# Eight of 22 up-projection chunks per layer as seven block products (Strassen's scheme), with the modulation columns of layer 0's MLP begun at the 15th chunk

## The chip, the cores and the metric

The kernel runs on one core of a Trainium2 chip. The metric is the device time of one execution in microseconds (us). TensorE (PE) multiplies matrices, VectorE (DVE) and ScalarE (ACT) do elementwise work, GpSimd (POOL) does little here, and SyncE (SP) issues nearly all DMAs. Each engine works through its own instruction list in order.

## What is computed

Two layers of a decoder trunk over 512 tokens of width 1024, all in float32. Each layer has an attention part with three head groups and a gated MLP. The change touches the MLP alone, whose reference is:

```python
h = rmsnorm(x, g_mlp[layer]) * (1.0 + scale2) + shift2
up = h @ w_up[layer]                               # 1024 -> 2 x 2816
u, g = up[..., :D_FF], up[..., D_FF:]
g = causal_depthwise_conv(g, conv_w[layer], conv_b[layer])     # width 3
x = x + gate2 * ((jax.nn.silu(g) * u) @ w_down[layer])
```

`shift`, `scale` and `gate` come from `mod = silu(c) @ w_mod[layer] + b_mod[layer]`: six times 1024 numbers per layer, which the kernel computes as 48 columns of 128.

## The kernel before, in words

Activations are held transposed: features on the 128 partitions, the 512 tokens along the free axis. `h` is eight tiles (k = 0 to 7) of 128 features. Every float32 operand of a matmul is split into a high part (`fp32r`, copied by ACT) and a low part (the rest, subtracted by DVE); a product is three matmuls, high x high (`hh,whi`), low x high (`hl,whi`), high x low (`hh,wlo`), in `mm3` (lines 250 to 253).

The up-projection runs over 22 chunks of 128 features. A chunk has a gate product (`pg`) and an up product (`pu`), each 8 k-tiles x 3 matmuls with 512 columns: 48 matmuls. The class `Weights` streams the weights in the order of the list `plan`: a DMA of 128x1024 into one of three `raww` buffers (line 148), ACT's copy to `whi` (L174), DVE's subtraction to `wlo` (L186), with two buffers for each of `whi` and `wlo`. `pump` is called between matmuls and starts these steps for the next weight. `post` (lines 888 to 906) finishes a chunk: ACT scales `pg` with the last tap of the convolution (L890), DVE adds the other taps (L892, L895), ACT applies SiLU (L898), DVE multiplies by `pu` (L902), and ACT and DVE split the result (L240, L242) for the down-projection (`dps`), which follows after chunk 21. Chunk 0 is different: it is computed in two halves of 256 tokens, between the steps that make `h` (L297, L299, L300).

In layer 0 another generator runs beside this: `mod_gen`, 56 columns (the last 8 of layer 0, the gate of its MLP, and all 48 of layer 1). One column is a 512 KB DMA (`rawm`, two buffers) and one DVE instruction of 128x1024 (L217). In the kernel before it starts with the MLP, and is moved on by `tick()` about four columns a chunk.

The generators only record the instructions. A scheduler then sets the order on each engine, by priorities and by its own estimates, so the order on an engine isn't that of the code.

## Time and profile before

| | us |
|---|---|
| median of three runs (1326.34 to 1332.99) | 1330.62 |
| the profiled execution | 1329.34 |
| its span, first to last instruction | 1327.6 |
| TensorE busy in the span | 1276.8 |
| DVE busy | 849.8 |
| ACT busy | 642.6 |
| layer 0's chunks, first `post` to last `post` | 318.89 to 553.98 |
| layer 1's chunks, first `post` to last `post` | 960.40 to 1178.43 |

The busy time of TensorE counts matmuls that overlap in the pipeline, so a matmul of 512 columns is listed with some 390 ns while the next one starts about 230 ns later. How fast TensorE goes is read from the starts. DVE and ACT instructions also start a little before the one ahead has ended, when nothing else holds them.

### The profile page before, as it was taken

To read this page: it belongs to the slowest core of one execution; us is meant where nothing else is said; L and a number is where in the kernel's file an instruction comes from. 1 tells how busy PE (TensorE), PEld (TensorE's weight loads), DVE (VectorE), ACT (ScalarE), POOL (GpSimd) and SP (SyncE) were. 2 spreads that over 40 slices of the span, in tenths; PEclk is the share of its full clock that TensorE was granted. 3 is DMA by queue.
4 is the path that set the end of the run, shared out by engine and by line. 5 is a ranking of instruction groups with operands and counts; after the bars stand their busy time and mean duration, and the time that the engine had idled before them with its cause. 6 is when DMAs were issued, how large, how long until landed. Compare 5 with 4: busy or idle time off the path is not lost.

```text
span 1327.6 us, 17720 instructions
## 1 busy us (share of the span) xinstructions
PE 1276.8 (96%) x6568; PEld 1057.6 (80%) x6568; DVE 849.8 (64%) x1600; ACT 642.6 (48%) x1158; POOL 22.1 (2%) x16
## 2 busy tenths in 40 slices
PE   4999999999999999999999999999999999999997
PEld 2788778787877788888898888878888888888886
DVE  6789999859888864422357788876754444443232
ACT  5667677745333333322346687785543333333231
POOL 5100000000000000000000000000000000000000
PEclk8999999999999999999999999999999999999999
DMA  9455464434888853333422334212133333332331
GB/s 370 167 165 157 145 189 136 132 99 144 260 270 265 271 170 95 92 88 99 129 87 96 96 100 141 77 43 90 48 111 97 95 95 95 96 91 88 104 99 64
DMA packets 56601, 174.39 MB, mean 131 GB/s; under 512 B 8130, under 2 KB 10450, under 8 KB 56516
## 3 DMA queue, kind: packets, MB, share of 16 engines
q1 hardware_dynamic: 55364, 172.16, 41.4%
q8 instruction: 52, 0.85, 0.3%
q10 hardware_dynamic: 1088, 1.05, 0.2%
q14 instruction: 33, 0.27, 0.1%
q0 software_dynamic: 64, 0.06, 0.0%
HBM read 159.41 MB, written 2.10 MB: 122 GB/s over the span
## 4 chain that ended last, share of the span: by engine, by line
PE 55%; DMA 7%; DVE 7%; ACT 4%; issue 3%; SPq 0%; DVEq 0%; ACTq 0%
DMA rawm<-in_wmod_dram 7%; PE dps L251 6%; PE dps L253 6%; PE dps L252 6%; PE pu L251 4%; PE pu L253 4%; PE pu L252 4%; PE pg L252 4%; PE pg L253 4%; PE pg L251 4%; PE qkps L251 1%; PE qkps L252 1%; PE qkps L253 1%; DVE rawm L217 1%; DVE wlo L186 1%
## 5 line engine op out<-in xcount | busy, mean ns | idle before, releaser
L186 DVE TENSOR_TENSOR wlo<-raww,whi 128x1024 fp32r<-128x1024 f32 (+3 forms) x188 | 224.4, 1194 | 240.9 <-ACT whi L174 236.4
L174 ACT ACTIVATE whi<-raww 128x1024 fp32r<-128x1024 f32 (+3 forms) x188 | 194.4, 1035 | 324.8 <-PE dps L252 137.7
L252 PE MATMUL pg<-hl,whi 128*128 128x512 f32 (+1 forms) x368 | 143.1, 389 | 1.5 <-DVE hl L300 1.5
L253 PE MATMUL pu<-hh,wlo 128*128 128x512 f32 (+1 forms) x368 | 141.3, 384 | 3.1 <-DVE wlo L186 3.0
L251 PE MATMUL pg<-hh,whi 128*128 128x512 f32 (+1 forms) x368 | 141.5, 385 | 1.6 <-ACT whi L174 1.6
L251 PE MATMUL pu<-hh,whi 128*128 128x512 f32 (+1 forms) x368 | 142.4, 387 | 0.1
L253 PE MATMUL pg<-hh,wlo 128*128 128x512 f32 (+1 forms) x368 | 140.9, 383 | 1.1 <-DVE wlo L186 1.1
L252 PE MATMUL pu<-hl,whi 128*128 128x512 f32 (+1 forms) x368 | 140.7, 382 | 0.0
L251 PE MATMUL dps<-mh,whi 128*128 128x512 f32 x308 | 121.5, 394 | 0.0
L253 PE MATMUL dps<-mh,wlo 128*128 128x512 f32 x308 | 121.5, 394 | 0.0
L252 PE MATMUL dps<-ml,whi 128*128 128x512 f32 x308 | 121.2, 393 | 0.0
L217 DVE CUSTOM_DVE_ANT_0 rawm<-rawm,scb,bm 128x1024 f32<-128x1024 f32 x80 | 102.4, 1281 | 23.3 <-DMA rawm<-in_wmod_dram 22.9
L654 ACT ACTIVATE e<-e,nm 128x256 f32<-128x256 f32 (+3 forms) x160 | 89.0, 557 | 33.1 <-DVE nm L641 29.5
L251 PE MATMUL qkps<-hh,whi 128*128 128x512 f32 x224 | 95.3, 426 | 4.7 <-ACT qk L434 4.1
L898 ACT ACTIVATE y<-y 128x512 f32<-128x512 f32 x44 | 27.8, 632 | 147.6 <-DVE y L895 147.6
L253 PE MATMUL qkps<-hh,wlo 128*128 128x512 f32 x224 | 90.2, 403 | 0.0
L252 PE MATMUL qkps<-hl,whi 128*128 128x512 f32 x224 | 90.1, 402 | 0.0
L253 PEld LDWEIGHTS pu<-hh,wlo 128*128 128x128 f32 x368 | 69.1, 188 | 22.2 <-DVE wlo L186 7.0
L641 DVE CUSTOM_DVE_ANT_0 e<-s,cst 128x256 f32<-128x256 f32 (+3 forms) x160 | 76.6, 482 | 11.1 <-PE s L628 3.4
L252 PEld LDWEIGHTS pg<-hl,whi 128*128 128x128 f32 x368 | 69.0, 188 | 17.7 <-DVE hl L300 3.2
L253 PEld LDWEIGHTS pg<-hh,wlo 128*128 128x128 f32 x368 | 69.0, 187 | 16.6 <-DVE wlo L186 1.9
L251 PEld LDWEIGHTS pg<-hh,whi 128*128 128x128 f32 x368 | 69.1, 188 | 16.0 <-ACT whi L174 2.0
(176 smaller groups left out, 2651.2 us busy)
## 6 DMA issues: line engine op xcount, KB each, us to landing
raww<-in_wup_dram SPq DMA_DIRECT2D x88, 512.0 KB
rawm<-in_wmod_dram SPq DMA_DIRECT2D x80, 512.0 KB
raww<-in_wqk_dram SPq DMA_DIRECT2D x32, 512.0 KB
raww<-in_wdown_dram SPq DMA_DIRECT2D x32, 512.0 KB
mu<-in_wmod_dram SPq DMA_DIRECT2D x16, 512.0 KB
raww<-in_wout_dram SPq DMA_DIRECT2D x16, 448.0 KB
raww<-in_wv_dram SPq DMA_DIRECT2D x12, 512.0 KB
raww<-in_wdown_dram SPq DMA_DIRECT2D x16, 384.0 KB
```

The costliest lines, as they stand in the source:

```text
L174: A.activation(out=h[:, 0:m], in_=self.raw[i][:, c:c + m], func=AF.Copy)
L186: V.tensor_tensor(out=lo[:, 0:m], in0=raw[:, c:c + m], in1=h[:, 0:m].bitcast(F32), op=ALU.subtract)
L217: V.tensor_tensor_reduce(out=raw, in0=raw, in1=scb, scale=1.0, scalar=bm[:, l, ci:ci + 1], op0=ALU.mult, op1=ALU.add, accum_out=dst)
L251: T.matmul(ps[:, c], w[0], rhs[0][:, c], start=first, stop=False, skip_group_check=True)
L252: T.matmul(ps[:, c], w[0], rhs[1][:, c], start=False, stop=False, skip_group_check=True)
L253: T.matmul(ps[:, c], w[1], rhs[0][:, c], start=False, stop=last, skip_group_check=True)
L641: anchor[0] = V.tensor_tensor_reduce(out=e[:, 0:n], in0=s[:, 0:n], in1=cst[:, mask + SEQ - n:mask + SEQ], scale=-scale, scalar=3e38, op0=A ...
L654: anchor[1] = A.activation(out=e[:, 0:n], in_=e[:, 0:n], func=AF.Exp, bias=nm, scale=-1.0, accum_out=den).ins
L898: last_silu[0] = A.activation(out=y, in_=y, func=AF.Silu).ins
```

## The change

For chunks 3, 4, 6, 7, 9, 10, 12 and 13 of each layer (`SCH`) the gate and the up weight of the chunk are taken as a 2 x 2 block matrix, A11 and A12 the two halves of the gate weight over k, A21 and A22 those of the up weight, and `h` as 2 x 2 blocks over k-half and token-half (`LO` and `HI`). Seven products of half size replace the eight. Each has 4 k-tiles x 3 matmuls with 256 columns, 84 matmuls in place of 48.

- The seven left factors are A11, A11+A21, A21+A22+A11, A22, A21+A22, A12, and A12+(A21+A22+A11), called f0 to f6 below. `form` makes each: DVE adds (`s3`, `s1`, `s2`, `s4`, L176), ACT's copy of the high part (L189), DVE's subtraction (L190). High and low part of a factor share one tile `wst`. The four buffers of `whi` and `wlo` are used in turn, so a factor needs the buffer of the factor four ahead of it.
- The right factors that are sums of blocks of `h` are made once a layer by `tforms`, from chunk 0 on: for each of four pairs of k-tiles two sums (`hf`, L998), four half-width differences (`td`, `te`, L1005), and two splits (`th`, `tl`, L306 and L308).
- `seven` runs the products P0 to P6 (with f0 to f6). Some are accumulated on top of others in the same half of a PSUM tile; copies of the parts in between are kept by ACT (`k1`, `k2`, L1038, L1040, L1042), and three DVE instructions join the rest (L1044, L1046, L1048). P0 is copied before P2 is added to it, P1 before P3, P2 before P4, and P4 is read by L1046 before P6 goes to the same half.
- Layer 0's `mod_gen` is no longer added at the start of the MLP but ahead of chunk 14 (`max(SCH) + 1`).

```diff
-        plan += [(wup[l, j], 1024, "wp") for j in range(2 * FC)]
+        for c in range(FC):
+            if c in SCH:
+                plan += [((wup[l, 2 * c + 1], wup[l, 2 * c]), f, "st") for f in range(7)]
+            else:
+                plan += [(wup[l, j], 1024, "wp") for j in (2 * c, 2 * c + 1)]
...
+        def form(self, i):
...
+            if f == 1:
+                add("s3", a11, a21)
+            elif f == 2:
+                add("s1", a21, a22)
+                add("s2", s["s1"], a11)
+            elif f == 6:
+                add("s4", a12, s["s2"])
...
+            t = wp.tile([128, 4 * VZ], F32R, tag=("whi", "wlo")[self.par], name="wst")
+            self.par ^= 1
+            A.activation(out=t[:, 0:512], in_=src, func=AF.Copy)
+            V.tensor_tensor(out=t[:, 512:1024], in0=src, in1=t[:, 0:512].bitcast(F32), op=ALU.subtract)
...
+        def tforms():
+            for kp in range(KC // 2):
+                a, b = h[kp], h[kp + KC // 2]
+                f = []
+                for hi, lo in (a, b):
+                    f.append(tmp("hf", "ev"))
+                    V.tensor_tensor(out=f[-1], in0=hi.bitcast(F32), in1=lo.bitcast(F32), op=ALU.add)
+                    yield
+                td, te = tmp("td", "ev"), tmp("te", "ev")
+                for out, p, q, op in ((td[:, LO], f[0][:, LO], f[0][:, HI], ALU.subtract),
+                                      (td[:, HI], f[0][:, HI], f[1][:, HI], ALU.subtract),
+                                      (te[:, LO], td[:, HI], f[0][:, LO], ALU.subtract),
+                                      (te[:, HI], f[1][:, LO], te[:, LO], ALU.add)):
+                    V.tensor_tensor(out=out, in0=p, in1=q, op=op)
+                    yield
...
+        def seven(c):
...
+            def prod(d, rhs, start=False):
+                w = W.use()
+                for k in range(KC // 2):
+                    hi, lo = w[:, 128 * k:128 * k + 128], w[:, 512 + 128 * k:640 + 128 * k]
+                    rh, rl = rhs(k)
+                    T.matmul(d, hi, rh, start=start and k == 0, stop=False, skip_group_check=True)
+                    T.matmul(d, hi, rl, start=False, stop=False, skip_group_check=True)
+                    T.matmul(d, lo, rh, start=False, stop=k == KC // 2 - 1, skip_group_check=True)
...
+            k1, k2 = tmp("k1", "e"), tmp("k2", "e")
+            prod(pg[:, HI], plain(0, LO), True)
+            A.activation(out=k1[:, LO], in_=pg[:, HI], func=AF.Copy)
+            prod(pu[:, LO], tform(1), True)
+            A.activation(out=k1[:, HI], in_=pu[:, LO], func=AF.Copy)
+            prod(pg[:, HI], tform(2))
+            A.activation(out=k2[:, LO], in_=pg[:, HI], func=AF.Copy)
+            prod(pu[:, LO], tform(3))
+            V.tensor_tensor(out=pu[:, LO], in0=pu[:, LO], in1=k2[:, LO], op=ALU.subtract)
+            prod(pg[:, HI], tform(0))
+            V.tensor_tensor(out=pu[:, HI], in0=k1[:, HI], in1=pg[:, HI], op=ALU.subtract)
+            prod(pg[:, LO], plain(1, LO))
+            V.tensor_tensor(out=pg[:, LO], in0=pg[:, LO], in1=k1[:, LO], op=ALU.add)
+            prod(pg[:, HI], plain(1, HI))
+            g = post(c, pg, [pu])
...
+            if l == 0 and c == max(SCH) + 1:
+                aux.append(mod_gen([(0, u) for u in range(40, 48)] + [(1, u) for u in range(48)], 200))
+            if c in SCH:
...
+                seven(c)
+                continue
             if c == 0:
...
+                aux.append(tforms())
                 continue
...
-                if l == 0:
-                    aux.append(mod_gen([(0, u) for u in range(40, 48)] + [(1, u) for u in range(48)], 200))
                 nst = layer_mlp(l, mp, nst)
...
+SCH = (3, 4, 6, 7, 9, 10, 12, 13)
```

What the scheduler makes of it is shown at three places of layer 0. Rows of the changed kernel have its own line numbers. In the names, the number behind a tile tells one buffer's use from another.

**DVE at the end of chunk 0, before.** Ahead of and behind the last low part of `h` (`hl_3506`) stand two modulation columns (L217), and then the weights of chunk 1.

```order
L297 SCALAR_TENSOR_TENSOR ht_3597<-x_98,scl_108,rstd_3363 128x256
L300 SCALAR_TENSOR_TENSOR hl_3497<-ht_3590,modc_107,hh_3496 128x256
L217 ISA rawm_3484,modc_107<-rawm_3484,scb_96,bm_102 128x1024
L217 ISA modc_107 128x1
L300 SCALAR_TENSOR_TENSOR hl_3506<-ht_3597,modc_107,hh_3505 128x256
L217 ISA rawm_3549,modc_107<-rawm_3549,scb_96,bm_102 128x1024
L217 ISA modc_107 128x1
L186 TENSOR_TENSOR wlo_3633<-raww_3628,whi_3632 128x1024
```

After:

```order
L366 SCALAR_TENSOR_TENSOR hl_3491<-ht_3578,modc_107,hh_3490 128x256
L998 TENSOR_TENSOR hf_3633<-hh_3368,hl_3369 128x512
L366 SCALAR_TENSOR_TENSOR hl_3500<-ht_3585,modc_107,hh_3499 128x256
L998 TENSOR_TENSOR hf_3642<-hh_3392,hl_3393 128x512
L1005 TENSOR_TENSOR td_3649<-hf_3633 128x256
L1005 TENSOR_TENSOR td_3649<-hf_3633,hf_3642 128x256
L1005 TENSOR_TENSOR te_3650<-td_3649,hf_3633 128x256
L240 TENSOR_TENSOR wlo_3621<-raww_3616,whi_3620 128x1024
```

The two modulation columns are gone; the first two sums of `tforms` (L998), and then three of its half-width steps, stand in their place ahead of the weight.

**DVE where chunk 2 ends, before.** The post-processing of chunk 2 (`y_3767`), the modulation columns and the up weight of chunk 3 (`wlo_3822`) take turns.

```order
L892 SCALAR_TENSOR_TENSOR y_3767<-pg_3725,cw_103,y_3767 128x511
L217 ISA rawm_3755,modc_107<-rawm_3755,scb_96,bm_102 128x1024
L217 ISA modc_107 128x1
L895 SCALAR_TENSOR_TENSOR y_3767<-pg_3725,cw_103,y_3767 128x510
L217 ISA rawm_3775,modc_107<-rawm_3775,scb_96,bm_102 128x1024
L217 ISA modc_107 128x1
L902 TENSOR_TENSOR y_3767<-y_3767,pu_3769 128x512
L186 TENSOR_TENSOR wlo_3822<-raww_3773,whi_3821 128x1024
L242 TENSOR_TENSOR ml_3826<-y_3767,mh_3825 128x512
```

After, up to the third factor of chunk 3 (`wst_3870` is f2, `wst_3873` f3, `wst_3907` f5; `tl_3849` and `tl_3853` are the last low parts of the right factors, the first for P1 and P4, the second for P2 and P3):

```order
L1005 TENSOR_TENSOR td_3837<-hf_3830,hf_3835 128x256
L190 TENSOR_TENSOR wst_3873<-raww_3733,wst_3873 128x512
L1005 TENSOR_TENSOR te_3838<-td_3837,hf_3830 128x256
L308 TENSOR_TENSOR ml_3843<-y_3783,mh_3842 128x512
L1005 TENSOR_TENSOR te_3838<-hf_3835,te_3838 128x256
L308 TENSOR_TENSOR tl_3849<-td_3837,th_3848 128x512
L176 TENSOR_TENSOR s1_3866<-raww_3733 128x512
L308 TENSOR_TENSOR tl_3853<-te_3838,th_3852 128x512
L176 TENSOR_TENSOR s2_3868<-s1_3866,raww_3735 128x512
L190 TENSOR_TENSOR wst_3907<-raww_3735,wst_3907 128x512
L176 TENSOR_TENSOR s4_3923<-raww_3735,s2_3868 128x512
L190 TENSOR_TENSOR wst_3870<-s2_3868,wst_3870 128x512
```

The last steps of `tforms` stand behind the end of chunk 2 (the product with `pu_3785` is just ahead of these rows), and f5 ahead of f2. On TensorE the products of this chunk stand in the order P0, P1, P3, P2, P4, P5, P6.

**ACT in a later pair (chunks 6 and 7), before.** The copies of weights (L174) and the post-processing of these chunks:

```order
L174 ACTIVATE whi_4118<-raww_4065 128x1024
L890 ACTIVATE y_4104<-pg_4061,cb_104,cw_103 128x512
L898 ACTIVATE y_4104<-y_4104 128x512
L174 ACTIVATE whi_4158<-raww_4110 128x1024
L240 ACTIVATE mh_4162<-y_4104 128x512
L174 ACTIVATE whi_4202<-raww_4150 128x1024
L890 ACTIVATE y_4188<-pg_4146,cb_104,cw_103 128x512
```

After, from f0 of chunk 7 (`wst_4287`; then f1, f2, f4, f3, f5) on. `pg_4197` is chunk 6, `pg_4338` chunk 7:

```order
L189 ACTIVATE wst_4287<-raww_4231 128x512
L189 ACTIVATE wst_4305<-s3_4303 128x512
L189 ACTIVATE wst_4327<-s2_4325 128x512
L189 ACTIVATE wst_4368<-s1_4323 128x512
L956 ACTIVATE y_4336<-pg_4197,cb_104,cw_103 128x512
L189 ACTIVATE wst_4348<-raww_4163 128x512
L1038 ACTIVATE k1_4340<-pg_4338 128x256
L1040 ACTIVATE k1_4340<-pu_4339 128x256
L189 ACTIVATE wst_4386<-raww_4231 128x512
L964 ACTIVATE y_4336<-y_4336 128x512
L1042 ACTIVATE k2_4341<-pg_4338 128x256
```

The copy of chunk 7's P0 (L1038) stands behind f4 of chunk 7, the first step of chunk 6's post-processing (L956) and f3. On TensorE, in the same place, chunk 7's P0 is parted: six of its matmuls stand ahead of chunk 6's P5 and six ahead of its P6. Before, a chunk's matmuls follow the chunk ahead without a break:

```order
L251 MATMUL pu_4106<-hh_3505,whi_4074 128x512
L252 MATMUL pu_4106<-hl_3506,whi_4074 128x512
L253 MATMUL pu_4106<-hh_3505,wlo_4075 128x512
L251 MATMUL pg_4146<-hh_3368,whi_4118 128x512
L252 MATMUL pg_4146<-hl_3369,whi_4118 128x512
L253 MATMUL pg_4146<-hh_3368,wlo_4119 128x512
```

After (`wst_4236` is f4 and `wst_4253` f5 of chunk 6, `wst_4287` f0 of chunk 7):

```order
L1024 MATMUL pg_4197<-tl_3849,wst_4236 128x256
L1025 MATMUL pg_4197<-th_3848,wst_4236 128x256
L1023 MATMUL pg_4338<-hh_3368,wst_4287 128x256
L1024 MATMUL pg_4338<-hl_3369,wst_4287 128x256
L1025 MATMUL pg_4338<-hh_3368,wst_4287 128x256
L1023 MATMUL pg_4338<-hh_3374,wst_4287 128x256
L1024 MATMUL pg_4338<-hl_3375,wst_4287 128x256
L1025 MATMUL pg_4338<-hh_3374,wst_4287 128x256
L1023 MATMUL pg_4197<-hh_3392,wst_4253 128x256
L1024 MATMUL pg_4197<-hl_3393,wst_4253 128x256
```

The part of P0 that is moved ahead needs f0 of chunk 7 while chunk 6 still has two products to come.

## Rows read from the trace of the kernel before

**Rows 1.** The page: busy time by engine, and TensorE's granted clock by slice.

```profile
PE 1276.8 (96%) x6568; PEld 1057.6 (80%) x6568; DVE 849.8 (64%) x1600; ACT 642.6 (48%) x1158; POOL 22.1 (2%) x16
...
PEclk8999999999999999999999999999999999999999
```

**Rows 2.** Timeline of ACT, layer 1: start, duration (us), engine, line, operation.

```profile
1045.47 0.76 ACT L890 ACTIVATE y<-pg,cb,cw 128x512 f32<-128x512 f32 x1
...
1056.55 0.76 ACT L890 ACTIVATE y<-pg,cb,cw 128x512 f32<-128x512 f32 x1
```

**Rows 3.** Timeline of TensorE: a chunk's end in layer 1, and half-width products.

```profile
1049.85 0.39 PE L253 MATMUL pu<-hh,wlo 128*128 128x512 f32 x1
1050.08 0.39 PE L251 MATMUL pg<-hh,whi 128*128 128x512 f32 x1
...
665.73 0.28 PE L251 MATMUL dps<-mh,wh 128*128 128x256 f32 x1
...
673.41 0.28 PE L253 MATMUL dps<-mh,wl 128*128 128x256 f32 x1
```

**Rows 4.** Timeline of DVE at three places; the brackets name what ended a wait.

```profile
1050.35 0.69 DVE L902 TENSOR_TENSOR y<-y,pu 128x512 f32<-128x512 f32 x1 [2.08 <-PE pu L253]
1051.15 1.23 DVE L186 TENSOR_TENSOR wlo<-raww,whi 128x1024 fp32r<-128x1024 f32 x1
1052.29 0.69 DVE L242 TENSOR_TENSOR ml<-y,mh 128x512 fp32r<-128x512 f32 x1
...
327.67 0.69 DVE L242 TENSOR_TENSOR ml<-y,mh 128x512 fp32r<-128x512 f32 x1
328.27 0.75 DVE L892 SCALAR_TENSOR_TENSOR y<-pg,cw,y 128x511 f32<-128x511 f32 x1
...
302.25 0.42 DVE L278 TENSOR_TENSOR sqacc<-sqacc,sq 128x256 f32<-128x256 f32 x1
302.59 0.48 DVE L300 SCALAR_TENSOR_TENSOR hl<-ht,modc,hh 128x256 fp32r<-128x256 f32 x1
```

**Rows 5.** Timeline of ACT: two starts in a row, and a copy that waited for TensorE.

```profile
326.40 0.61 ACT L240 ACTIVATE mh<-y 128x512 fp32r<-128x512 f32 x1
326.92 0.76 ACT L890 ACTIVATE y<-pg,cb,cw 128x512 f32<-128x512 f32 x1
...
1050.05 1.06 ACT L174 ACTIVATE whi<-raww 128x1024 fp32r<-128x1024 f32 x1 [1.06 <-PE pu L252]
```

**Rows 6.** Groups by line and shape: ACT's half-width copy from PSUM (busy us, mean ns).

```profile
L378 ACT ACTIVATE vv<-vps 128x256 fp32r<-128x256 f32 x32 | 10.6, 379 | 2.9 <-PE vps L406 2.6
```

**Rows 7.** Windows, last columns clock, DMA share, GB/s: a weight's transfer ends.

```profile
1055.50:1056.00 0.50, 0.50 (x4) 0.41 (x3) 0.00 (x0) 0.42 (x1) 0.00 (x0) 1.00 0.12 33
```

**Rows 8.** Timelines of DVE, then TensorE, in chunk 0 of layer 0.

```profile
304.56 1.28 DVE L217 CUSTOM_DVE_ANT_0 rawm<-rawm,scb,bm 128x1024 f32<-128x1024 f32 x1
...
315.76 1.29 DVE L217 CUSTOM_DVE_ANT_0 rawm<-rawm,scb,bm 128x1024 f32<-128x1024 f32 x1
...
316.96 0.49 DVE L300 SCALAR_TENSOR_TENSOR hl<-ht,modc,hh 128x256 fp32r<-128x256 f32 x1
...
306.30 0.39 PE L252 MATMUL pg<-hl,whi 128*128 128x256 f32 x1 [0.62 <-DVE hl L300]
317.51 0.38 PE L252 MATMUL pg<-hl,whi 128*128 128x256 f32 x1 [0.63 <-DVE hl L300]
```

**Rows 9.** Timeline of ACT, layer 0: first step of `post` of chunks 4 and 15.

```profile
359.64 0.76 ACT L890 ACTIVATE y<-pg,cb,cw 128x512 f32<-128x512 f32 x1
...
487.50 0.77 ACT L890 ACTIVATE y<-pg,cb,cw 128x512 f32<-128x512 f32 x1
```

**Rows 10.** TensorE's timeline in attention, and windows (busy by engine, then granted clock).

```profile
136.87 0.50 PE L251 MATMUL qkps<-hh,whi 128*128 128x512 f32 x1 [2.13 <-ACT qk L434]
...
137.50:138.00 0.50, 0.50 (x6) 0.50 (x5) 0.50 (x1) 0.00 (x0) 0.00 (x0) 0.70 0.81 311
...
141.00:141.50 0.50, 0.50 (x4) 0.41 (x3) 0.35 (x2) 0.42 (x2) 0.00 (x0) 0.88 0.37 148
```

More of the change, by code (lines that the diff above doesn't have):

```diff
@@ L142, in __init__ @@
             self.pt = None
-        def dma(self, upto):
-            while self.nd < min(upto, len(plan)):
-                src, n, at = plan[self.nd]
+            self.loads, self.live, self.sums, self.par = [], set(), {}, 0
+            for i, (src, n, at) in enumerate(plan):
+                if at != "st":
+                    self.loads.append((i, src, n))
+                elif n == 0:
+                    self.loads += [(i, s, 1024) for s in src]
+        def dma(self, upto):
+            while self.nd < len(self.loads) and self.loads[self.nd][0] < upto:
+                i, src, n = self.loads[self.nd]
+                old = self.nd - 3
+                if old in self.live and "st" in (plan[i][2], plan[self.loads[old][0]][2]):
+                    return
@@ L199, in use, with ahead @@
             return cols
+        def ahead(self):
+            cost = {"st": 1, "wp": 2}
+            j, room = self.nu, 4 - cost.get(plan[self.nu - 1][2], 2)
+            while j < len(plan) and cost.get(plan[j][2], 2) <= room:
+                room -= cost.get(plan[j][2], 2)
+                j += 1
+            return j
         def pump(self, q):
+            st = any(p[2] == "st" for p in plan[self.nu - 1:self.nu + 1])
+            upto = self.ahead() if st else self.nu + 1
             if q == 0:
-                self.dma(self.nu + 2)
+                self.dma(self.nu + (8 if st else 2))
             elif q == 1:
-                self.hi(self.nu + 1)
+                self.hi(upto)
             elif q == 2:
-                self.lo(self.nu + 1)
+                self.lo(upto)
     W = Weights()
@@ L922, in layer_mlp @@
             W.pump(q)
+        LO, HI = HALVES
+        tf = []
+        def tforms():
[13 more added lines that the diff above has]
+                    yield
+                res = []
+                for t in (td, te):
+                    hi, lo = pair_tiles(mp, "m", "t")
+                    yield from split_gen(t, hi, lo)
+                    res += [(hi[:, LO], lo[:, LO]), (hi[:, HI], lo[:, HI])]
+                tf.append(res)
@@ new lines, in seven, with plain, tform @@
+        def seven(c):
+            pg = mm.tile([128, SEQ], F32, tag="mm", name="pg")
+            pu = ps_s.tile([128, SEQ], F32, tag="s", name="pu")
+            def prod(d, rhs, start=False):
[6 more added lines that the diff above has]
+                    T.matmul(d, lo, rh, start=False, stop=k == KC // 2 - 1, skip_group_check=True)
+                    W.pump(k)
+                    if k % 2:
+                        tick()
+            def plain(half, cc):
+                return lambda k: tuple(t[:, cc] for t in h[k + half * KC // 2])
+            def tform(j):
+                return lambda k: tf[k][j]
+            k1, k2 = tmp("k1", "e"), tmp("k2", "e")
[13 more added lines that the diff above has]
+            g = post(c, pg, [pu])
+            next(g)
+            aux.append(g)
@@ L925, in layer_mlp @@
             box = []
+            if l == 0 and c == max(SCH) + 1:
+                aux.append(mod_gen([(0, u) for u in range(40, 48)] + [(1, u) for u in range(48)], 200))
+            if c in SCH:
+                while any(g.__name__ == "tforms" for g in aux):
+                    tick()
+                seven(c)
+                continue
             if c == 0:
```

35 lines of the change are left out of this document (31 added, 4 removed).

## The prediction, made before the changed kernel ran

> **What bounds the kernel now.** I read the page first: TensorE is busy for 1276.8 of 1327.6 us at full granted clock in nearly every slice, and DVE has 849.8, ACT 642.6 [rows 1]. So TensorE's own work is the bound, and a saving there counts as long as nothing else takes its place. In layer 1 the first step of `post` comes every 11.08 us, from 1045.47 to 1056.55 [rows 2]. Two matmuls of 512 columns start 0.23 us apart [rows 3], and 48 of them are those 11.08 us: between plain chunks TensorE waits for nothing. DVE and ACT are hidden there. The question is whether they stay hidden.
>
> **TensorE's saving.** The trace has the new shape already, in the last product of the down-projection: 66 matmuls of 256 columns, the first start at 665.73, the last at 673.41, so 7.68 / 65 = 0.118 us each [rows 3]. A Strassen chunk has 84: 9.93 us, against 11.08. That is 1.15 us a chunk and 18.4 us for 16 chunks.
>
> The Trainium skill ("TensorE: Matmul & The Clock Gate", Back-to-back issue gap) gives N/2.4 + 2.5 ns between starts when the array is warm; by it a chunk would go from 10.4 to 9.2 us and the 16 would save an estimated 19 us. The trace has both shapes slower (0.231 and 0.118 us) and decides; the difference is too small to matter.
>
> **What DVE and ACT get to do.** On DVE an instruction of 128x512 takes 0.69 us, but the next one starts 0.60 us after it (327.67 to 328.27); one of 128x1024 starts its successor after 1.14 us, one of 128x256 after 0.34 [rows 4]. A Strassen chunk has 4 sums and 7 subtractions (11 x 0.61 = 6.7), 3 half-width joins (1.0), and the post-processing of four instructions (2 x 0.67 + 2 x 0.61 = 2.6): 10.3 us, where TensorE needs 9.93. A plain chunk has 2 x 1.14 + 2.6 = 4.9 of 11.08. Two Strassen chunks and the plain one behind them are 25.5 of 30.9 us. DVE fits on average, but inside a pair it has no air. ACT has 7 copies at 0.52 [rows 5], three half-width ones (at most 0.38 [rows 6]) and `post`: some 6.5 us. So it isn't work that decides, but the order, which I followed instruction by instruction. A handover costs little: DVE reads `pu` 0.27 us after the next group's first matmul has started (1050.35 against 1050.08) [rows 3, 4], and ACT's copy that waits for the matmul ahead of a chunk's last one starts at 1050.05, before the last one is through [rows 3, 5], so I take 0.2 us for it. TensorE itself loses about 0.1 us more when it starts again.
>
> **A later pair (three a layer).** Count from TensorE's start of the first chunk. Its P0 to P4 end at 7.1. Then the order has six matmuls of the second chunk's P0, whose low part DVE makes behind f6 of the first chunk (6.1), the join of P3 (6.45) and `s3` (7.05): ready at 7.7, wanted at 7.35, so 0.45 us with the restart. The second wait is at the second chunk's P2, which is added to the half that holds P0 and must wait for ACT's copy of it (L1038). The order puts that copy behind the first step of the first chunk's `post`, which needs P6 (end 11.8, seen at 12.0), and behind f3: 12.0 + 0.66 + 0.53 + 0.38 = 13.6, where TensorE is through with P1 at 13.2. With the restart 0.55. All else I found in time, some by 0.1 us only (the low part of the next gate weight). So a pair loses 1.0 us of its 2.3. Six pairs: 6.0. The bounds are 0 (the margins of 0.3 us fall the other way) and 2.5 (the close ones fail too).
>
> The weights' DMAs are hidden: a buffer is free with the subtraction's end (1051.15 + 1.23 = 1052.4 [rows 4]), and the transfer that it lets start ends before 1056.0 [rows 7]: some 3.4 us, where the order leaves 4 or more.
>
> **The first pair of a layer.** Here `tforms` is late. From the weight subtraction of chunk 1 to the last low part for P1 (`tl_3849`) DVE has 4 instructions at 1.14, 6 at 0.67, 13 half-width ones at 0.34 and 23 at 0.61: 27.0 us with hardly a gap, starting 0.7 us ahead of chunk 1. That ends at 27.1 with waits for results just written, which is 5.0 us into chunk 3 (chunk 3 starts at 22.15), and P1's last k-pair wants it at 2.5. P1 ends at 5.5 in place of 2.84: 2.65 lost. P3, next on TensorE, waits for `tl_3853` until 6.2: 0.7. P2 waits for f2, which stands on DVE behind `s2`, f5 and `s4`, and f5 needs the buffer that P1 frees: 8.7 in place of 7.7, so 1.0. P4 waits for the copy `k2` behind a copy that waits for a DMA: 0.4. The second chunk's P2: 0.6. Five restarts: 0.5. Sum 5.85 a layer, 11.7 for two; bounds 3 (only P1 waits) and 8 a layer.
>
> In attention TensorE once waited 2.13 us, and 0.8 us after it was back the granted clock went to 0.5 (1.2 of 2.4 GHz), from 137.7 to 141.1 by the windows of 0.70 and 0.88 [rows 10]. The waits in chunk 3 are of that length. Half clock for 3.4 us of which a part is waiting anyway costs about 1.0 us a layer (0 to 3): 2.0.
>
> **Chunk 0.** In layer 0 DVE sets the pace there: the modulation columns at 304.56 and 315.76 each stood ahead of the low part of `h` that TensorE then waited for, 0.62 and 0.63 us [rows 8]. Both go; in place of the second stands one sum of 0.61. I take 1.5 us gained (0.6 to 2.4). In layer 1 the same sum is new and costs about 0.7 with the steps behind it. Net -0.8.
>
> **The modulation columns.** They are 1.28 us of DVE each [rows 8]. Before, chunks 4 to 15 took 127.86 us [rows 9] where 11 x 11.08 = 121.88: 6.0 us lost, none of it in the first four chunks. After, the same load lies on chunks 14 to 21 and on the down-projection, where DVE has air. It should cost 1.3 (if it needs four chunks to build up again) to 5.2; I take 3.0. The 56 DMAs go along on SP's queue: in chunks 1 to 13 it then carries weights alone, in 14 to 21 it is as full as it was in 1 to 8, and the gate columns, the first eight, are there long before the down-projection uses them. At the seam a column stands ahead of the last factor of chunk 13 and of the gate weight of chunk 14: 1.8 us. Net -6.0 + 3.0 + 1.8 = -1.2.
>
> **The sum.** -18.4 + 11.7 + 6.0 + 2.0 - 0.8 - 1.2 = -0.7 us. Against the profiled execution (1329.34, which is the span and 1.7 us around it) that is 1328.6. The median of the runs shown is 1.3 us higher, so I say 1330: the gain of the multiplications is spent on waits.
>
> **Rival 1, faster: only P1 of the first pairs waits.** If DVE and ACT hand over a few tenths sooner than I count, the waits of the later pairs close, and in the first pairs P2 and P3 find their parts ready once P1 is through: -18.4 + 2 x 2.75 - 0.8 - 1.2 = -15, so 1316. For it: the waits of the later pairs are 0.35 and 0.45 us, less than my error over ten steps. Against it: on DVE f2 stands behind three instructions that can't start before P1 has ended.
>
> **Rival 2, slower: DVE is the bound.** If an instruction held DVE for its whole 0.69 us, a Strassen chunk would cost it 11.7 us, each pair would lose some 1.5 us more (18 instructions a chunk at 0.08), and the first pairs 3.6 us more each (46 x 0.08): +9 + 7, so 1346. It decides as soon as starts are more than about 0.65 us apart. Against it: 0.60 in the trace [rows 4]; for it: those are few, and nearly every new subtraction waits for a copy by ACT just ahead of it.
>
> The Trainium skill speaks for this rival ("VectorE: DVE Perf Modes", The DRAIN you can't avoid): after each instruction the pipe is emptied before the next one starts. The trace disagrees for the rows that I could read (0.60 between starts of an instruction of 0.69 us); the same page says that an instruction that is not held starts earlier.
>
> **Rival 3: the half-width matmuls don't cost half.** If each took as long as a weight load, which is 1057.6 / 6568 = 0.161 us in the mean [rows 1], a Strassen chunk would take 13.5 us, 2.4 more than a plain one: 16 x 2.4 = +39 in place of -18.4, so 1387. The matmuls of 0.118 us stand against it [rows 3]: they, too, had a load each.
>
> **Chances.** The forecast, within 0.5% (which is about what a measurement of this kernel can tell from no change): 0.51. Faster by more, rival 1 and what lies between: 0.25. Slower by more, rival 2 and a longer first pair: 0.22, rival 3: 0.02. Some two in ten lie beyond the bounds of the single terms taken together (the first pairs -5.7 to +4.3, the later ones -6 to +9, the rest some 3 either way, which don't all fall on one side), so the range goes most of the way to the first two rivals: 1319 to 1341.
>
> **What would show it.** In the changed kernel's profile: matmuls of 256 columns 0.118 us apart in chunks 3 to 13; TensorE idle some 5 us in chunk 3 of each layer, ended by `tl`, then by `wst`, with half clock behind it; in each later pair an idle time ended by DVE `wst` and one by ACT `k1`; from one plain chunk to the next 32 us in place of 33.2; no half-microsecond waits for `wlo` left in chunks 5 to 11 of layer 0, and some in chunks 18 to 21. I am wrong if the wait in chunk 3 is under 3 us, or if later pairs take 31 or over 33 us.

## The result and the profile after

The changed kernel takes 1337.92 us (median of 7 runs, 1336.38 to 1340.41), the kernel before in the same session 1330.22. The ratio is 1.0067, 95% interval 1.0055 to 1.0079: slower, by 7.7 us between the two medians (7 to 10 us by the interval), where I had forecast no change. The time is inside the range; the direction isn't what I said.

The page of the changed kernel (busy us by engine, the slices, the chain that ended last) answers to [rows 1]:

```profile
span 1335.9 us, 19340 instructions
PE 1273.8 (95%) x7144; PEld 1078.7 (81%) x7144; DVE 967.3 (72%) x1856; ACT 697.0 (52%) x1302; POOL 22.2 (2%) x16
DVE  6789999859888788876357788876897876443232
GB/s 369 172 167 156 138 183 151 125 89 80 79 96 95 111 243 259 267 274 229 128 98 95 92 101 142 71 49 90 49 94 95 95 95 111 95 91 87 103 99 63
PE 57%; DVE 18%; DMA 10%; ACT 9%; issue 5%; SPq 1%; POOL 0%; DVEq 0%; ACTq 0%; POOLq 0%
DMA rawm<-in_wmod_dram 8%; PE dps L317 4%; PE dps L319 4%; PE dps L318 4%; PE pg L1023 3%; PE pg L1025 3%; PE pg L319 3%; PE pg L317 3%; PE pg L318 2%; DVE rawm L283 2%; PE pg L1024 2%; PE pu L317 2%; PE pu L318 2%; PE qkps L317 2%; PE pu L319 2%
```

TensorE's busy time fell by 3 us only, where 16 chunks at 1.15 us would be 18.4: matmuls at half clock and the slow restart behind a wait count as busy too. The transfers of the modulation columns (243 to 274 GB/s) moved from slices 11 to 14 to slices 15 to 18, and they still lead the chain (7% before, 8% now).

**Where the 8.3 us between the two profiled spans lie.** The marks to read them by are the first step of `post`, one a chunk on ACT ([rows 2, 9] before, L956 now), and in the down-projection the addition of each finished block to `x` on DVE. Plain chunk to plain chunk was 33.24 us; layer 0 and layer 1 now show (start, length, engine, line):

```profile
372.01 0.76 ACT L956 ACTIVATE y<-pg,cb,cw 128x512 f32<-128x512 f32 x1
389.11 0.78 ACT L956 ACTIVATE y<-pg,cb,cw 128x512 f32<-128x512 f32 x1 [0.83 <-PE pg L1025]
404.36 0.76 ACT L956 ACTIVATE y<-pg,cb,cw 128x512 f32<-128x512 f32 x1
...
1021.28 0.76 ACT L956 ACTIVATE y<-pg,cb,cw 128x512 f32<-128x512 f32 x1
1053.67 0.76 ACT L956 ACTIVATE y<-pg,cb,cw 128x512 f32<-128x512 f32 x1
...
1086.08 0.76 ACT L956 ACTIVATE y<-pg,cb,cw 128x512 f32<-128x512 f32 x1
```

A middle pair with its plain chunk takes 32.35, 32.39 and 32.41 us (one takes 32.79). So the products do gain where nothing else is in the way. Layer 0's up-projection ends 3.07 us earlier than before (550.91 against 553.98). Then the additions to `x` in its down-projection, after and before:

```profile
577.60 0.75 DVE L378 SCALAR_TENSOR_TENSOR x<-dps,modc,x 128x512 f32<-128x512 f32 x1
593.78 0.75 DVE L378 SCALAR_TENSOR_TENSOR x<-dps,modc,x 128x512 f32<-128x512 f32 x1
611.53 0.75 DVE L378 SCALAR_TENSOR_TENSOR x<-dps,modc,x 128x512 f32<-128x512 f32 x1
629.41 0.75 DVE L378 SCALAR_TENSOR_TENSOR x<-dps,modc,x 128x512 f32<-128x512 f32 x1
640.92 0.75 DVE L378 SCALAR_TENSOR_TENSOR x<-dps,modc,x 128x512 f32<-128x512 f32 x1 [2.12 <-PE dps L319]
656.24 0.75 DVE L378 SCALAR_TENSOR_TENSOR x<-dps,modc,x 128x512 f32<-128x512 f32 x1 [2.08 <-PE dps L319]
...
689.11 0.48 DVE L378 SCALAR_TENSOR_TENSOR x<-dps,modc,x 128x256 f32<-128x256 f32 x1
```

```profile
574.07 0.75 DVE L312 SCALAR_TENSOR_TENSOR x<-dps,modc,x 128x512 f32<-128x512 f32 x1 [2.12 <-PE dps L253]
589.39 0.75 DVE L312 SCALAR_TENSOR_TENSOR x<-dps,modc,x 128x512 f32<-128x512 f32 x1 [2.08 <-PE dps L253]
...
683.49 0.48 DVE L312 SCALAR_TENSOR_TENSOR x<-dps,modc,x 128x256 f32<-128x256 f32 x1
```

Before, a block takes 15.32 us. After, the blocks up to 629.41 come 16.18, 17.75 and 17.88 us apart, and as soon as the columns are through (the last starts at 628.20) they take 15.32 again. (The addition is a DVE instruction and is itself held up there: the one at 640.92 follows the late one at 629.41 by 11.51 us. So only the sum over the stage counts.) From the last `post` to the last addition it was 129.51 us and is now 138.20: **8.69 us are lost in layer 0's down-projection**, more than the whole difference. (That is one execution: in e5 below, with the same order of transfers, it is 11.45.) What stands there on DVE (the number in brackets is the idle time ahead, and what ended it):

```profile
600.16 0.95 DVE L240 TENSOR_TENSOR wlo<-raww,whi 128x768 fp32r<-128x768 f32 x1
601.88 1.29 DVE L283 CUSTOM_DVE_ANT_0 rawm<-rawm,scb,bm 128x1024 f32<-128x1024 f32 x1 [0.76 <-DMA rawm<-in_wmod_dram]
603.09 0.08 DVE L283 DVE_READ_ACCUMULATOR2_ANT modc<- 128x1 f32 x1
605.01 1.28 DVE L283 CUSTOM_DVE_ANT_0 rawm<-rawm,scb,bm 128x1024 f32<-128x1024 f32 x1 [1.84 <-DMA rawm<-in_wmod_dram]
606.23 0.08 DVE L283 DVE_READ_ACCUMULATOR2_ANT modc<- 128x1 f32 x1
606.34 0.17 DVE L293 SCALAR_TENSOR_TENSOR scl<-modc,gM 128x8 f32<-128x8 f32 x1
606.45 1.23 DVE L240 TENSOR_TENSOR wlo<-raww,whi 128x1024 fp32r<-128x1024 f32 x1
```

Two columns stand between one weight subtraction and the next. Each waits for its own transfer, and the subtraction, whose weight has long landed (ACT copied it at 600.88), waits behind them. The waits of 551 to 640 us (total, times, longest):

```profile
DVE rawm L283 <- DMA rawm<-in_wmod_dram: 22.7, 22, 2.1
PE dps L319 <- DVE wlo L240: 4.9, 7, 2.0
```

The longest of TensorE's waits, and a matmul behind it:

```profile
607.73 0.50 PE L319 MATMUL dps<-mh,wlo 128*128 128x512 f32 x1 [2.01 <-DVE wlo L240]
...
610.37 0.63 PE L318 MATMUL dps<-ml,whi 128*128 128x512 f32 x1
```

Over 605 to 621 us the granted clock is 0.89. The starts of the matmuls account for the loss: the seven waits cost 6.9 us with their restarts, and after the longest the starts are 0.43 us apart instead of 0.23 until 612.4, which is another 1.7. DVE itself had air, as I had said: it is busy for 60.26 of these 90 us.

### The profile page after: what moved, and what is told of

Its sections match the earlier page's. It is cut to its first block, busy times and chain, and to the rows that moved or that the text cites. A ratio compares the mean times of both kernels' runs of the same rounds, so it can differ in the third digit from the quotient of the medians.

```text
span 1335.9 us, 19340 instructions
## 1 busy us (share of the span) xinstructions
PE 1273.8 (95%) x7144; PEld 1078.7 (81%) x7144; DVE 967.3 (72%) x1856; ACT 697.0 (52%) x1302; POOL 22.2 (2%) x16
## 4 chain that ended last, share of the span: by engine, by line
PE 57%; DVE 18%; DMA 10%; ACT 9%; issue 5%; SPq 1%; POOL 0%; DVEq 0%; ACTq 0%; POOLq 0%
DMA rawm<-in_wmod_dram 8%; PE dps L317 4%; PE dps L319 4%; PE dps L318 4%; PE pg L1023 3%; PE pg L1025 3%; PE pg L319 3%; PE pg L317 3%; PE pg L318 2%; DVE rawm L283 2%; PE pg L1024 2%; PE pu L317 2%; PE pu L318 2%; PE qkps L317 2%; PE pu L319 2%
## 5 line engine op out<-in xcount | busy, mean ns | idle before, releaser
L240 DVE TENSOR_TENSOR wlo<-raww,whi 128x1024 fp32r<-128x1024 f32 (+2 forms) x156 | 185.0, 1186 | 139.4 <-ACT whi L224 122.6
L224 ACT ACTIVATE whi<-raww 128x1024 fp32r<-128x1024 f32 (+2 forms) x156 | 160.5, 1029 | 236.1 <-PE dps L318 119.9
L318 PE MATMUL pg<-hl,whi 128*128 128x512 f32 (+1 forms) x240 | 93.0, 387 | 0.5 <-DVE hl L366 0.4
L319 PE MATMUL pu<-hh,wlo 128*128 128x512 f32 (+1 forms) x240 | 90.6, 378 | 1.3 <-DVE wlo L240 1.3
L317 PE MATMUL pu<-hh,whi 128*128 128x512 f32 (+1 forms) x240 | 91.4, 381 | 0.0
L318 PE MATMUL pu<-hl,whi 128*128 128x512 f32 (+1 forms) x240 | 90.5, 377 | 0.0
L319 PEld LDWEIGHTS dps<-mh,wlo 128*128 128x128 f32 x308 | 58.3, 189 | 21.8 <-DVE wlo L240 8.2
L470 PE MATMUL vps<-whi,hh 128*128 128x256 f32 (+1 forms) x256 | 74.7, 295 | 0.1
L471 PE MATMUL vps<-wlo,hh 128*128 128x256 f32 (+1 forms) x256 | 72.1, 283 | 0.0
L472 PE MATMUL vps<-whi,hl 128*128 128x256 f32 (+1 forms) x256 | 72.0, 283 | 0.0
```

The source lines that it names most:

```text
L224: A.activation(out=h[:, 0:m], in_=self.raw[i][0][1][:, c:c + m], func=AF.Copy)
L240: V.tensor_tensor(out=lo[:, 0:m], in0=raw[:, c:c + m], in1=h[:, 0:m].bitcast(F32), op=ALU.subtract)
L317: T.matmul(ps[:, c], w[0], rhs[0][:, c], start=first, stop=False, skip_group_check=True)
L318: T.matmul(ps[:, c], w[0], rhs[1][:, c], start=False, stop=False, skip_group_check=True)
L319: T.matmul(ps[:, c], w[1], rhs[0][:, c], start=False, stop=last, skip_group_check=True)
L470: T.matmul(d, h[k][0][:, b], wc[0], start=go, stop=False, skip_group_check=True)
```

## The experiments

My theory after the comparison: the place of the columns costs the time, not the products, and it costs by the round of a column buffer. Of the ratios, each is against the kernel before, run on the same chip.

**One part alone: the products (e1).** The columns begin with the MLP again.

```
-            if l == 0 and c == max(SCH) + 1:
-                aux.append(mod_gen(...))
...
                 anchor[0] = gate[0]
+                if l == 0:
+                    aux.append(mod_gen(...))
```

> The seven products as in the changed kernel, but layer 0's modulation columns begin with the MLP again, as in the kernel before. Theory (the columns' new place is what costs): the products cost what layer 1 of the changed kernel shows, +2.5 us from chunk 0 to chunk 21, in either layer, and the columns lose their old 6 us in the up-projection; the down-projection of layer 0 is as before, 15.3 us an output block: 1330.2 + 5.0 = about 1335, and 1333 to 1337. Rival (VectorE cannot carry sums and columns at once): pairs 6/7 to 12/13 of layer 0 take over 34.5 us from plain chunk to plain chunk instead of 32.4, and the whole is 1339 or more.

1373.19 us, ratio 1.0313 (1.029 to 1.0335). My theory failed here, and the rival is right: from plain to plain chunk layer 0 takes 43.92, 41.41 and 41.89 us. One row of e1's windows by stage (stretch, its length, then busy us of PE, PEld, DVE, ACT; this one is the first pair) and one of the changed kernel's later pairs, without columns:

```profile
338.00:390.00 52.00, 38.93 (x217) 33.70 (x216) 47.41 (x82) 18.67 (x34) 0.00 (x0) 0.87 0.56 177
```

```profile
372.00:467.00 95.00, 92.00 (x632) 83.45 (x631) 74.86 (x123) 51.31 (x92) 0.00 (x0) 1.00 0.32 100
```

DVE is full there, 47.41 of 52 us, and in e1's later pairs it is busy for 80.04 of the 85.30 us from 390.3 to 475.6. With products alone it is at 74.86 of 95, and a column every 2.9 us would add 1.28 of each 2.9. So the two edits aren't independent: columns beside products cost some 40 us, and moving them was needed for the products.

**The other part alone: the move (e2).**

```
             ms.append(None)
             box = []
+            if l == 0 and c == 14:
+                aux.append(mod_gen(...))
...
                 anchor[0] = gate[0]
-                if l == 0:
-                    aux.append(mod_gen(...))
```

> The kernel before with one edit: layer 0's modulation columns begin at the 15th chunk; no products. Theory (the place alone costs): chunks 0 to 14 are freed (-6.0 us, and -1.5 us in chunk 0), chunks 19 to 21 lose 1.9 us and the down-projection 8.7 us, as in the changed kernel: +3.1 us, about 1333, with three idle stretches of half a microsecond or more before wlo in the down-projection. Rival (the loss in the down-projection is a backlog that the products' sums leave on VectorE): the move does what the prediction said, -6.0 - 1.5 + 3.0 us, about 1325.7.

1336.56 us, 1.0044 (1.0032 to 1.0056): slower without any product. From chunk 0 to 15 it takes 162.63 us where the kernel before took 168.61, so the 6.0 us came back as forecast; from 15 to 21 it loses 2.06, and from the last `post` to the last addition it takes 143.20 us, 13.7 more than before. The rival (a backlog of the products) is out. The time lies above my 1333, since the down-projection lost more than in the changed kernel (e2's profiled execution, 1338.86, is 2.3 us above its median, so 13.7 is on the high side). By the ratios (1.0067 against 1.0044) the changed kernel's 16 product chunks add some 3 us to the move's 6.

**Without the first pair (e3).**

```
-SCH = (3, 4, 6, 7, 9, 10, 12, 13)
+SCH = (6, 7, 9, 10, 12, 13)
```

> The changed kernel with six product chunks a layer (6, 7, 9, 10, 12, 13); chunks 3 and 4 are plain. Theory (the first pair of a layer pays for the combinations of the input being late, +4.1 and +3.9 us against plain chunks): they are long ready at chunk 6, so both losses go and the other pairs stay at 32.4 us from plain to plain: 1337.9 - 8.0 = about 1330. Rival (whichever pair comes first pays, for filling the row of factors): the loss moves to chunk 6, and two pairs' gain of 0.85 us is lost beside: about 1339.6.

1330.05 us, 1.0005 (0.9991 to 1.0019), as the theory said: 8 us less than the changed kernel. The pair 6/7 takes the usual time (367.49 to 399.87 is 32.38; before it as the second pair 32.35):

```profile
367.49 0.76 ACT L956 ACTIVATE y<-pg,cb,cw 128x512 f32<-128x512 f32 x1
384.58 0.78 ACT L956 ACTIVATE y<-pg,cb,cw 128x512 f32<-128x512 f32 x1 [0.81 <-PE pg L1025]
395.18 0.78 ACT L956 ACTIVATE y<-pg,cb,cw 128x512 f32<-128x512 f32 x1 [1.08 <-PE pg L1025]
399.87 0.77 ACT L956 ACTIVATE y<-pg,cb,cw 128x512 f32<-128x512 f32 x1
```

So it isn't being first that costs a pair, but `tforms` being late: in e3 its last low part starts at 343.73, some 13 us ahead of chunk 6, and TensorE doesn't wait for `th` or `tl`.

**Half the transfer, the same work on DVE (e4).**

```
+        late = l == 1 and ci >= 16
-        nc.sync.dma_start(out=raw, in_=wmod[l, ci])
+        nc.sync.dma_start(out=raw[:, 0:512] if late else raw, in_=wmod[l, ci, :, 0:512] if late else wmod[l, ci])
...
+            for q in range(2):
+                V.tensor_tensor_reduce(out=raw[:, 0:512], in0=raw[:, 0:512], in1=scb[:, 0:512], ...)
```

> The changed kernel, but layer 1's modulation columns from the 17th on (24 of them run in the down-projection of layer 0) load half of their rows, 256 KB instead of 512 KB, and VectorE multiplies this half twice (two instructions of 512 instead of one of 1024), so that its work doesn't shrink; these columns' values are therefore other ones. Theory (a multiplication that waits for its own transfer holds up the weight subtraction behind it on VectorE): the transfers land early, VectorE no longer waits for them, and of the 8.7 us lost in the down-projection at most 2 stay: about 1331. Rival (VectorE has too much to do there): nothing changes, 1337 to 1339.

1330.48 us, 1.0004 (0.9993 to 1.0015). DVE does as much, and the down-projection loses 1.3 us only: 130.85 us from the last `post` to the last addition. (Chunks 18 to 21 still lose 1.8.) What DVE has to do there isn't the cause; what it waits for is.

**Spreading the late columns: one that changed nothing (e5), and one that did (e9).** e5 put two empty steps behind each column from layer 1's 25th on.

```
                 yield
+            for _ in range(2 if (l, u) >= (1, 24) else 0):
+                yield
```

> The changed kernel; the columns that run in the down-projection (layer 1's from the 25th on) are spread: one every 6 steps of the order instead of every 4, so one in 4.2 us instead of 2.8; nothing is left out. Theory (each of the two column buffers goes round from transfer to multiplication to the next transfer in about 5 us, which is nearly the 5.5 us that two columns have, so VectorE stands before late columns with the weight subtraction behind): with 8.3 us for two columns the waits go, the down-projection of layer 0 loses at most 1.5 us instead of 8.7: about 1330.5. Rival (every column costs its 0.36 us there, by what it takes from VectorE and the transfers): the same 24 columns cost the same, 1337 to 1339.

1339.31 us, 1.0073 (1.0055 to 1.0091). By its own terms that is the rival's result, but the run decides nothing: the order of the transfers on SP's queue is that of the changed kernel, letter for letter. In the up-projection a column is kept behind the last `y` of the chunk before; in the down-projection nothing renews this anchor, so a column goes as soon as a buffer is free, whenever the code asks for it. e9 renews it at each weight subtraction (from layer 1's 21st column on, two steps more):

```
-                    V.tensor_tensor(out=lo[:, 0:m], ...)
+                    sub = V.tensor_tensor(out=lo[:, 0:m], ...)
+                    if down[0]:
+                        anchor[0] = sub.ins
```

The transfers in SP's order from the last up-projection weights on (U, D: a weight of the up- or down-projection; m: a column), for the changed kernel (and e5), then for e9:

```
UmmUmmDmmDmmDmmDmmDmmDmmDmmDmmDmmDmmDmmDmmDmmDmmDmmDDDDDDDDD
UmmUmmDmmDmmDmmDmDmmDmDmDmDmmDmDmDmDmDmmDmDmDmDmmDmDmDmDmDDm
```

> The changed kernel, nothing left out; from layer 1's 21st column on, one column every 6 steps, and in the down-projection each column is kept behind the last weight subtraction, so that the spacing now stands in the transfer queue's order: after the first three weights 1.3 columns between two weights instead of 2 (in the run that was to be spread before, the order did not change at all). Theory (two columns and a weight take a round of some 5.9 us, and the down-projection's three weights of a block take 15.3 us, 5.1 each): a loss of 0.8 us at each of the first weights, none behind: the down-projection loses about 2.5 us instead of 8.7, 1331.5 in all. Rival (each column costs 0.36 us wherever it runs): 1337 to 1339.

1329.17 us, 1.0002 (0.9989 to 1.0014). Same columns, same bytes, same DVE work, and the last column 31 us later: the down-projection takes 130.47 us (0.96 lost), and the waits of 551 to 640 us are

```profile
DVE rawm L285 <- DMA rawm<-in_wmod_dram: 6.2, 4, 2.4
...
PE dps L323 <- DVE wlo L240: 0.4, 1, 0.4
```

**The kernel before with spread columns (e6).** The same two empty steps for all 56 columns, without products.

> The kernel before (no products; columns from the start of layer 0's MLP), with the same spreading for all 56 columns: 336 steps, to the end of the up-projection, instead of 224. Theory (the round of the two buffers): the 6.0 us that chunks 4 to 15 of layer 0 lose in the kernel before go, and every chunk takes 11.08 us: about 1324. Rival (a price per column): the 6 us are spread out and stay, 1330.

1324.03 us, 0.9955 (0.9938 to 0.9973). From chunk 2 on each chunk of layer 0 takes 11.08 us. So the 6 us that the kernel before lost in chunks 4 to 15 go with the spacing too: not a price per column.

**A third column buffer (e10).** From the 15th chunk on every third column goes to two tiles of 512.

```
+        third = mrx[0] if mrx and l == 1 and ci % 3 == 2 else None
+        if third:
+            for q in range(2):
+                nc.sync.dma_start(out=third[q], in_=wmod[l, ci, :, 512 * q:512 * q + 512])
```

> The changed kernel with a third column buffer from the 15th chunk of layer 0 on (two tiles of 512 columns each; every third column is loaded and multiplied in two halves); nothing left out. Theory (the round of two buffers, some 5 us from transfer to multiplication to the next transfer, is what is too long, not the rate of the transfers, since the start of the kernel moves 410 GB/s where this stretch moves 260 to 280): with three buffers the round has 8 us, and of the 8.7 us at most 3 stay: 1330 to 1332. Rival (the transfers' rate is the limit): the same bytes take as long, 1337 to 1339.

1330.50 us, 1.0004 (0.9993 to 1.0014). Chunks 19 to 21 lose nothing now (11.08 each), the down-projection 1.9 us. The rate of the transfers is therefore not the limit, and the windows of 548 to 608 us say so directly (last column GB/s; the changed kernel, then e10):

```profile
548.00:608.00 60.00, 55.46 (x234) 43.07 (x233) 44.27 (x64) 16.85 (x20) 0.00 (x0) 1.00 0.82 265
```

```profile
548.00:608.00 60.00, 58.96 (x252) 46.81 (x252) 48.26 (x84) 15.97 (x19) 0.00 (x0) 1.00 0.87 293
```

With the third buffer more is moved, and the last column is multiplied at 611.05 instead of 628.20. One reservation: the third buffer also altered SP's order (half a column to three behind a weight, about two in the mean), so it isn't the buffer alone; but it put no fewer columns behind a weight.

**Columns ahead of the products and behind them (e7).** Six product chunks a layer, 24 columns from the MLP's start, 32 from the 15th chunk, at the old pace.

> Six product chunks a layer (6, 7, 9, 10, 12, 13), and layer 0's columns on either side of them at the old pace of one every 4 steps: 24 from the MLP's start (chunks 0 to 5), 32 from the 15th chunk (to the 22nd), none in the down-projection. Theory: the same as the run with six product chunks, 1330.0, less its 11 us in the down-projection, more some 3 us in chunks 0 to 5 (1.5 in chunk 0, 1.5 in chunks 4 and 5): about 1322. Rival (VectorE, with columns in chunks 0 to 5, brings the combinations of the input late again): the pair 6/7 takes 2 to 4 us longer, 1325 or more.

1341.86 us, 1.0096 (1.0073 to 1.0119). The rival is right and too small: columns and `tforms` share DVE in chunks 0 to 5, the columns run late into the products, and chunk 6 comes 23.50 us after chunk 5 and chunk 7 24.64 after chunk 6, where 17.1 and 10.6 are usual; one wait for `wlo` there holds TensorE for 7.6 us, shorter ones for copies, joins and factors for 7.2 more. The part that I was after held: with hardly a column left in the down-projection its blocks take 15.32 to 15.34 us.

**What is best (e8, e11, e12).** e8 has products in layer 1 alone and spread columns from the MLP's start in layer 0. e11 has six product chunks in both layers, eight spread columns in chunks 0 to 5 and the others from the 15th chunk as in e9, every 5 or 6 steps. e12 is e11 with the eight columns from chunk 3.

> Products in layer 1 alone (six chunks), layer 0 as before with the columns spread (one every 6 steps from the MLP's start). Theory: about 1324 from the spreading, less 1 to 2.6 us of layer 1's three pairs: 1321.4 to 1323. Rival (the products of layer 1 gain nothing against plain chunks in the total, only in their own stretch): no faster than the spread columns alone.

1321.32 us, 0.9944 (0.9927 to 0.9961). That is in the theory's range. The interval overlaps e6's, but the traces show the gain: layer 1's chunks, first to last `post`, take 226.65 us where e6's take 229.13.

> Six product chunks a layer (6, 7, 9, 10, 12, 13), eight columns of layer 0 spread over its first chunks, the other 48 from the 15th chunk, one every 5 or 6 steps, kept behind the weight subtraction in the down-projection; nothing left out. Theory: the run with six product chunks took 1330.0 and lost 11 us in layer 0's down-projection and 1.3 in chunks 20 and 21; spaced columns give back all but 1 to 2 of these: 1318 to 1320, faster than the spread columns without products in layer 0 (1324.0, and 1321.3 with products in layer 1). Rival (the products gain nothing once the columns are spaced, since their sums fill VectorE): 1321 to 1324.

1319.92 us, 0.993 (0.9912 to 0.9949); all 56 columns, and TensorE waits not once for `wlo` in the down-projection, which takes 129.56 us. The median is in the theory's range; the interval also reaches the rival's 1321.

> The run with six product chunks and spaced columns (1319.9), with one edit: the eight columns that ran in chunks 0 to 5 of layer 0 begin at chunk 3 instead of chunk 0, one every 6 steps; nothing left out. Theory (chunks 0 to 2 have the combinations of the input on VectorE, and the early columns cost 2.8 us there, 23.9 us from chunk 0's end to chunk 2's... against 21.0 in the first three pitches without columns): about 1317.5. Rival (the 2.8 us were TensorE's clock after the waits at chunk 1, which comes in some runs and not in others, whatever is on VectorE; or the columns now delay the pair 6/7): no change within 1 us, 1319 to 1321.

1318.37 us, 0.992 (0.99 to 0.9939), about 11 us faster than the kernel before and 19.5 faster than the changed one. The pair 6/7 takes 32.40 us (368.49 to 400.89): the columns of chunks 3 to 5 delay nothing. (The 2.8 us of the expectation are right, its bracket isn't: from the first `post` to the fourth e11 takes 32.59 us, e12 29.76.) Whether e12's 1.5 us against e11 come from the columns, the times can't say, as the intervals overlap. The traces give a part: in e11's chunk 1 a column stands ahead of the weight on DVE and TensorE waits 1.36 us for `wlo`, in e12 0.60. The rest of that chunk's 2.3 us is half clock behind this wait (see the last section), which may or may not follow.

Of the 11 us the spacing alone gives 5 (e6). The products of layer 1 give 2.5 more (e8), those of layer 0 0.9 (its chunks take 228.18 us in e12, 229.12 in e8): together 3.4, where 12 chunks at 1.15 us would save 13.8 without any wait. Another 1.1 comes from layer 0's chunk 0 without columns (first `post` at 317.00 against 318.09); the rest I can't place.

## Why the prediction failed, step by step

By the profiled executions, in us against the plain pitch, layer 0 / layer 1:

| Step | forecast | measured |
|---|---|---|
| chunks 0 to 2 | -1.5 / +0.7 | -2.8 / -0.4 |
| first pair | +4.55 / +4.55 | +4.1 / +3.8 |
| pairs 6/7 and 9/10 together | -2.6 / -2.6 | -1.3 / -1.7 |
| pair 12/13 with the seam behind it | +0.5 / -1.3 | +1.1 / +0.7 |
| columns gone from chunks 0 to 14 | -6.0 | -6.0 |
| columns in chunks 15 to 21 and the down-projection | +3.0 | +10.6 |
| end of layer 1 | 0 | +0.2 |
| sum | -0.7 | +8.3 |

Of the 9.0 us between forecast and measurement 7.6 are in one term, the columns' new place. The misses of the others, -3.6 and +5.0, nearly cancel, which is luck.

- **The step that failed** is the last term of the modulation columns: "on the down-projection, where DVE has air. It should cost 1.3 (...) to 5.2; I take 3.0". It cost 1.9 + 8.7 = 10.6. I sized it by DVE's occupancy, and carried over "the same load" as a loss per column. The loss goes by something else: two columns and a weight take a round of 5.7 to 5.8 us. Before, the 34 steps from the column at 371.8 to that at 470.9 us are 5.83 a pair; in the changed kernel's down-projection the 25 steps from 557.2 to 628.2 are 5.68. The order puts two columns behind each weight. An up-projection weight gives them 5.54 us, so each loses some 0.3; a down-projection block gives three weights 15.32, which is 5.11, so each loses some 0.6, and 28 of the columns run after the up-projection: 14 pairs, 8.0 us, where 8.69 was measured. By the round of before alone it would have been 10. Both numbers were in that trace: I had the loss (6.0 in 11 chunks) and didn't ask what it was a loss of. e9 and e10 show that it goes when the columns stand further apart or have a third buffer, e4 that it goes when the transfer is shorter.
- **The first pair** came out within a microsecond of its sum, in part by luck. TensorE's waits in chunk 3 of layer 0:

```profile
342.84 0.38 PE L1023 MATMUL pu<-th,wst 128*128 128x256 f32 x1 [0.45 <-ACT th L306]
344.43 0.39 PE L1024 MATMUL pu<-tl,wst 128*128 128x256 f32 x1 [1.21 <-DVE tl L308]
344.65 0.28 PE L1025 MATMUL pu<-th,wst 128*128 128x256 f32 x1
345.40 0.38 PE L1023 MATMUL pu<-th,wst 128*128 128x256 f32 x1 [0.47 <-ACT k L1040]
```

  `th` and `tl` instead of `tl` alone, 2.1 us with the restarts where I had 2.65, and behind them waits for the copies `k` (0.47 and 0.24; in the second chunk 0.48) where I had put waits for `wst`. The clock fell as forecast: granted 0.67 over 345.4 to 350.5 us. I had named under 3 us of waiting in chunk 3 as what would prove me wrong. The idle times listed there come to 2.37, so that sign was met; by the starts of the matmuls, which also show the restarts, it is 3.4. With the second chunk's wait that is 4.1 us where I had 5.85; half clock (1.6 instead of 1.0) and small irregular starts make up most of the difference. e9 shows the pair at full clock (1.00 in its windows): there the wait for f2 that I had counted is in both layers,

```profile
351.38 0.39 PE L1030 MATMUL pg<-th,wst 128*128 128x256 f32 x1 [0.64 <-DVE wst L190]
```

  and the pair loses 3.3 and 3.4 us instead of 4.1 and 3.8. Here, at half clock, that wait doesn't show. e3 shows that the pair's loss goes when `tforms` is through in time.
- **The later pairs** have the two waits that I named, 0.18 to 0.25 before `wst` and 0.22 to 0.25 before `k`, some 0.95 with the restarts by the starts of the matmuls, where I had 1.0. Yet a pair gains 0.85 (once 0.45) and not 1.3. In the pair 6/7 of layer 0, where the trace has all 216 matmuls, the other 0.5 lies in starts that are late without a listed wait: 0.3 from 395.1 to 396.0, where the plain chunk's first two matmuls stand among the last product's, and 0.1 at each of two other changes. I had no such term.
- **The seam** behind pair 12/13 came in layer 0 as priced: a wait of 1.54 us for `wlo` at 462.44, where I had 1.8. In layer 1, without columns, the row is 2.0 us off all the same, and some 1.1 of it is a wait in chunk 13:

```profile
1098.57 0.63 ACT L189 ACTIVATE wst<-raww 128x512 fp32r<-128x512 f32 x1 [2.11 <-DMA raww<-in_wup_dram]
1099.25 0.39 PE L1023 MATMUL pg<-hh,wst 128*128 128x256 f32 x1 [0.89 <-ACT wst L189]
```

  A weight's transfer, which I had called hidden, isn't always: e1, e9 and e10 have this wait too (0.72 to 0.76), e4 and e5 don't. Of the rest 0.45 is the smaller gain of any later pair, and 0.43 is the mark that I read by: ahead of a product chunk the first step of `post` comes sooner (chunk 2: 0.50 us after the matmul that follows its gate product, 334.70 against 334.20; before, 0.93, 337.48 against 336.55). So in each layer 0.43 us belongs to the table's fourth row instead of its first.
- **256 columns cost half**: starts are 0.118 us apart in chunk 3 (340.34 to 341.05 is six of them). Rival 3 is out. Rival 2 (DVE the bound) didn't come true in the changed kernel, and e1 shows how near it is. Its price was too low by its own numbers: 18 instructions at 0.08 us are 1.4 us a chunk, so 2.9 a pair and not 1.5. Rival 1 was out with the waits of the later pairs and the half clock in chunk 3.
- The half-microsecond waits for `wlo` left chunks 5 to 11 and came to chunks 19 to 21, as said.

The Trainium skill ("DMA: Bandwidth & Descriptors", Anatomy of one DMA — SWDGE (gpsimd) path) splits a transfer into a fixed 2.0 us and bytes at 436 GB/s, given for another issuing path than this one. By it a column of 512 KB alone would be an estimated 3.2 us from issue to signal. The trace agrees in kind: the column issued at 586.89 is multiplied at 590.60, 3.7 us later, with other transfers under way.

## What to carry to other kernels

A load that is moved takes its buffers and its order along: ask of the place it leaves what the loss there was a loss of (here a round of 5.83 us for two transfers against 5.54 us of work), and compare that with the time the new place gives it (5.11). An engine with air by its busy time can still hold up everything behind an instruction that waits for its own transfer. And two edits that each look hidden can need the same engine: try each alone.
